# A hybrid RWKV-7 and attention step: norms, blocks, low-rank products and output products of the scan done in another way

## The chip, the cores and the metric

The program runs on one core of one Trainium2 chip. The metric is device time in microseconds (us) of one execution. The core has five engines, each with an instruction stream of its own that it works through in order: TensorE (PE in the profile; its weight loads are PEld) for matrix products into PSUM, VectorE (DVE), ScalarE (ACT), GpSimd (POOL, here called Pool) and SyncE (SP), which issues all the DMAs of this kernel.

## The reference, cut to what matters

Layer 0 is a bidirectional RWKV-7 scan beside a gated convolution, layer 1 is grouped-query attention. Of 1280 tokens 1024 are latent and 256 are context. What the change touches is the scan with its norms, and the mean squares of the other norms.

```python
def rwkv_scan(S0, r, w, k, v, kk, a, reverse):
    def step(S, inp):
        r_t, w_t, k_t, v_t, kk_t, a_t = inp
        sk = jnp.einsum('bhvk,bhk->bhv', S, kk_t)
        S = (S * w_t[:, :, None, :] - sk[..., None] * (kk_t * a_t)[:, :, None, :]
             + v_t[..., None] * k_t[:, :, None, :])
        return S, jnp.einsum('bhvk,bhk->bhv', S, r_t)
...
    w_log = -jax.nn.softplus(-(w0 + jnp.einsum('bldr,drc->bldc', jnp.tanh(lw), lw2))) - 0.5
    a = jax.nn.sigmoid(a0 + jnp.einsum('bldr,drc->bldc', la, la2))
    kk = kk / jnp.maximum(jnp.sqrt(jnp.sum(kk * kk, axis=-1, keepdims=True)), 1e-12)
    S_f, y_f = rwkv_scan(S0[:, 0], r_h, w_h[:, :, 0], k_h[:, :, 0], v_h, kk, a_h[:, :, 0], False)
    S_b, y_b = rwkv_scan(S0[:, 1], r_h, w_h[:, :, 1], k_h[:, :, 1], v_h, kk, a_h[:, :, 1], True)
    y = y_f + y_b
    mean = jnp.mean(y, axis=-1, keepdims=True)
    var = jnp.mean(jnp.square(y - mean), axis=-1, keepdims=True)
    y = ((y - mean) * lax.rsqrt(var + GN_EPS)).reshape(B, L, A_WIDTH) * lnx_g + lnx_b
```

## The kernel before, in words

**A planner orders the instructions.** Every part of the work is a Python generator. Before each piece it yields the engine that it needs and the tiles, rings of buffers (`Ring`) and conditions for which it waits. `Loom.run` (line 330) keeps a model of each engine's clock, with prices from `COST` (line 39), `TABLES` (line 46, the sets of ScalarE's functions; a change of set is priced at 1.28 us) and `Loom.issued` (line 246). It takes the first generator in the order of `PRECEDENCE` (line 48) whose turn has come by that model. The order of each engine's stream is thus fixed when the kernel is built. A price is used for that order alone; what an instruction waits for on the chip is set by semaphores. In the prices, two products whose 64 rows lie in different halves of the array run together when they are of type float32r.

**The stretch with the scan.** `fill` (line 1394) makes the first input projection: 34 column blocks, each as products of three kinds (high and low halves of activations and weights, `mm<-h_hi,whi` and the like in the profile) over three blocks of tokens. `evacuate` takes the results out of PSUM through ScalarE, VectorE and Pool; `norm_k` (line 715) normalises the keys in groups of 256 tokens, 20 times in all: square on ScalarE, a product with `ones2` on TensorE, Sqrt on ScalarE, a floor and a reciprocal on VectorE, a multiply, and a DMA to `rkv_d`.

The scan itself has 20 steps: four pairs of heads, and for each pair four groups of 256 latent tokens in both directions and one of the context. Each step passes through these generators:

- `prepare` (line 895): the low-rank products (`iv<-lor,lw`, for the two directions `d` one after the other, each in the single `iv` bank of PSUM, each with the parts `z` for decay and gate), tanh, cumulative decay, and the scaled operands on Pool.
- `interact` (line 981): products of the operands among themselves (`wk<-s,bk`, in both `wk` banks), masks, and the matrices to be inverted, which go through DRAM.
- `solve` (line 1041): the inverse of sixteen 32x32 triangles by 62 small VectorE operations on `acc` and `tmp`. Two solvers take the even and the odd steps; `all_solved` (line 1430) starts step n+2 only when the chain of step n is done.
- `merge` (line 1066): transposes the values, then joins the 32x32 inverses to 64x64 ones. The first blocks are transposed by 16 products of 32x32 with `ident` (`iv<-ident,w`), copied to `t11`, and followed by two more rounds of small products (`iv<-t,nn`, `iv<-w,zz`), each with a copy.
- `chain` (line 1121): four chunks of 64 tokens in sequence, both directions and both heads together. A chunk issues the product of state and keys (`ch<-hv,s`), copies it to `xs`, issues the first part of the outputs (`py<-s,hv`) and, on Pool, the decayed state `hg`; then the product with the inverse (`ch<-xs,w`), a copy to `hv`, the state product (`ch<-hv,tbk`), four VectorE operations that make the next state, the second part of the outputs (`py<-br,hv`), and the copy or addition of the outputs to `y`. Each direction has a `py` bank of its own; there are two.
- `finish` and `close_groups` (line 1241), 20 times: mean and variance of `y` by products with `ones2`, Sqrt on ScalarE, reciprocal on VectorE, and the gate.

**The other norms.** `norm_x` (line 1296) for the input rows, `rsqrt_mean` (line 1747) after each layer and `normed_heads` (line 1840) for queries and keys use a Sqrt on ScalarE and a reciprocal on VectorE, on 1 to 8 columns.

In the profile nearly every line is L145, that of the helper that records operations; tiles tell them apart. A float32 product stands as two records, so 160 records of `iv<-lor,lw` are 80 products.

Of the kernel before, what the change touches and what calls it, by code (L numbers as in the profile page):

```python
# [10 lines left out]
F32R = mybir.dt.float32r  # L11
AF = mybir.ActivationFunctionType
ALU = mybir.AluOpType
# [28 lines left out]

WINDOW = 3.413


TABLES = {AF.Tanh: 0, AF.Exp: 0, AF.Sqrt: 1, AF.Silu: 2}
# [70 lines left out]
class Loom:  # L117
# [128 lines left out]
    def issued(self, e, name, a, k, r):  # L246
# [9 lines left out]
        if e == "T":  # L256
# [3 lines left out]
            else:  # L260
                dur = max(0.054, n * (1 if ins[0].dtype == F32R else 4) / 2400.0)
                if ins[0].dtype == F32R and ins[0].partition_size() == 64:
# [20 lines left out]
        elif e == "G":  # L283
            dur = COST[e][0] + n * COST[e][1]
# [83 lines left out]
def hybrid_step(  # L368
# [34 lines left out]
    V.memset(eps_t[:, 0:1], EPS)  # L403
    V.memset(eps_t[:, 1:2], GN_EPS)

# [309 lines left out]
    def norm_k(p, b, f, done):  # L715

        t0, n, _ = BLK[b]
        for h in range(0, n, GRP):
# [176 lines left out]
    def prepare(x):  # L895
# [11 lines left out]
        for d in range(2):  # L907
            yield "T", x.lor, lw2, iv_ps
            pz = iv_ps.take()
            for z in range(2):  # L910
                T.matmul(pz[:, z * GRP:(z + 1) * GRP], lw2[HH[d], z, :], x.lor[HH[d], z, :], start=True, stop=True)
            for z in range(2):
# [3 lines left out]
            iv_ps.release(pz)  # L916
# [149 lines left out]
    def merge(x):  # L1066
# [54 lines left out]
    def chain(x):  # L1121
# [33 lines left out]
        yield "T", x.hv[:, :, :, 0], x.s[0], x.s[1], x.w, ch_ps  # L1155
        pc = ch_ps.take()
        for i in range(4):
# [46 lines left out]
            for d in range(2):  # L1204
# [4 lines left out]
                if d == 1:  # L1209
                    ysl = ysl[:, ::-1]  # L1210
# [1241 lines left out]
```

## Time and profile before

| | |
|---|---|
| median of 3 runs | 2253.53 us (2251.32 to 2257.36) |
| profiled execution | 2253.86 us |
| its span, first to last instruction | 2252.2 us |
| busy TensorE / VectorE / ScalarE / Pool | 2052.1 / 1471.9 / 1052.1 / 1012.0 us |
| mean granted TensorE clock | 0.951 |
| tables loaded by ScalarE | 56 in all, 71.8 us |

The table is for the whole execution; the stages have different limits, so the rows below are by stage and by tile. Busy times of an engine are the union of its instructions' times. The time of an instruction begins when its engine takes it up; where it then waits for a port, the wait is part of its time.

### The profile page before, as it was taken

How to read it: one execution, taken by the hardware profiler on the slowest of the kernel's cores; microseconds unless marked ns; L12 is line 12 of the kernel's file. 1: busy time of each engine (PE TensorE's matmuls, PEld its weight loads, DVE VectorE, ACT ScalarE, POOL GpSimd, SP SyncE). 2: the span in 40 equal slices, each digit the busy share in tenths (PEclk: the TensorE clock that was granted, in tenths of full speed). 3: DMA queues.
4: the chain of work that ended last, by engine and by line, in shares of the span. 5: the costliest groups of instructions: out<-in, count | busy, mean ns of one | idle time of the engine just before them, and what ended most of it. 6: DMA issues, size and time to landing. Idle time of an engine off the chain costs nothing.

```text
span 2252.2 us, 42921 instructions
## 1 busy us (share of the span) xinstructions
PE 2052.1 (91%) x15306; PEld 1411.7 (63%) x15306; DVE 1471.9 (65%) x3483; ACT 1052.1 (47%) x2476; POOL 1012.0 (45%) x1152
## 2 busy tenths in 40 slices
PE   4998889798988988998979999999999999999898
PEld 1486666576666666666657788888454545454487
DVE  2346878948888886868645733552877777775443
ACT  3446556645665556554435632221354444444422
POOL 2434344333344343333224321430487777888622
PEclk7999899999998999999889999999799999999899
DMA  7834344324433333342345633323321211102243
GB/s 271 305 98 131 98 105 131 85 68 114 102 97 103 99 96 101 85 111 54 86 153 185 206 111 88 99 87 107 82 53 48 60 42 38 43 28 71 58 131 108
DMA packets 337818, 232.86 MB, mean 103 GB/s; under 512 B 163890, under 2 KB 289860, under 8 KB 335556
## 3 DMA queue, kind: packets, MB, share of 16 engines
q1 hardware_dynamic: 337604, 230.12, 35.0%
q8 instruction: 120, 1.97, 0.4%
q14 instruction: 94, 0.77, 0.1%
HBM read 166.95 MB, written 57.75 MB: 100 GB/s over the span
## 4 chain that ended last, share of the span: by engine, by line
PE 39%; DVE 9%; DMA 5%; issue 3%; ACT 1%; POOL 1%; SPq 1%; DVEq 0%; POOLq 0%; ACTq 0%
PE mm L145 21%; PE pv L145 8%; PE wk L145 5%; PE py L145 4%; DVE mx L145 3%; DVE rz L145 1%; DVE zs L145 1%; DMA rz<-rz_d 1%; PE ch L145 1%; DVE tmp L145 1%; SPq L145 1%; DVE acc L145 1%; DMA rz_d<-rc 1%; DMA rc<-rz 0%; DVE hv L145 0%
## 5 line engine op out<-in xcount | busy, mean ns | idle before, releaser
L145 POOL TENSOR_TENSOR zs<-zs,pe 128x512 f32<-128x512 f32 x275 | 366.8, 1370 | 34.1 <-ACT pe L145 32.1
L145 PE MATMUL mm<-h_hi,whi 128*128 128x512 f32 (+1 forms) x816 | 336.5, 412 | 4.3 <-ACT whi L145 4.1
L145 PE MATMUL mm<-h_hi,wlo 128*128 128x512 f32 (+1 forms) x816 | 299.3, 367 | 8.1 <-DVE wlo L145 7.2
L145 PE MATMUL mm<-h_lo,whi 128*128 128x512 f32 (+1 forms) x816 | 298.7, 366 | 0.0
L145 POOL TENSOR_TENSOR wlo<-wraw,whi 128x128 fp32r<-128x128 f32 x228 | 111.4, 494 | 246.0 <-ACT whi L145 205.8
L145 PE MATMUL pv<-pe,v_sb 128*64 128x512 f32 (+1 forms) x832 | 200.4, 604 | 0.0
L145 PEld LDWEIGHTS mm<-h_hi,whi 128*128 128x128 f32 x816 | 159.9, 196 | 49.5 <-issue 12.2
L145 PEld LDWEIGHTS mm<-h_hi,wlo 128*128 128x128 f32 x816 | 160.1, 196 | 37.1 <-DVE wlo L145 10.0
L145 DVE TENSOR_TENSOR acc<-acc,tmp 128x60 f32<-128x60 f32 (+23 forms) x620 | 168.0, 273 | 20.8 <-issue 2.9
L145 PE MATMUL mm<-wts,omh 128*128 128x512 f32 x648 | 166.6, 410 | 7.6 <-ACT wts L145 4.0
L145 PEld LDWEIGHTS mm<-h_lo,whi 128*128 128x128 f32 x816 | 161.0, 197 | 14.4
L145 PE MATMUL mm<-wts,h_hi 128*128 128x512 f32 x480 | 151.1, 396 | 0.0
L145 POOL TENSOR_TENSOR hg<-hv,gc 64x128 f32<-64x128 f32 x152 | 65.1, 428 | 185.0 <-DVE hv L145 173.9
L145 PEld LDWEIGHTS mm<-wts,omh 128*128 128x128 f32 x648 | 122.9, 194 | 38.0 <-ACT wts L145 5.3
L145 ACT ACTIVATE whi<-wraw 128x128 fp32r<-128x128 f32 x272 | 80.2, 305 | 78.2 <-DMA wraw<-in_w_in_e_dram 40.3
L145 DVE TENSOR_REDUCE mx<-mm 128x1 f32<-128x512 f32 (+1 forms) x138 | 89.7, 660 | 36.7 <-PE py L145 12.6
L145 DVE SCALAR_TENSOR_TENSOR hv<-ch,gc,hg 64x64 f32<-64x64 f32 x288 | 81.3, 282 | 49.3 <-PE ch L145 42.2
L145 POOL TENSOR_TENSOR xr<-xr,og 128x512 f32<-128x512 f32 x40 | 54.6, 1364 | 128.4 <-DVE og L145 93.3
L145 PEld LDWEIGHTS pv<-pe,v_sb 128*64 128x64 f32 x832 | 51.6, 139 | 93.9 <-issue 82.3
L145 DVE TENSOR_REDUCE mx<-py 128x1 f32<-128x512 f32 (+1 forms) x138 | 89.6, 660 | 28.7 <-PE mm L145 13.0
L145 DVE TENSOR_TENSOR tmp<-acc,nra 128x31 f32<-128x31 f32 (+7 forms) x320 | 90.1, 282 | 27.4 <-DMA acc<-eye_d 17.7
L145 ACT ACTIVATE pe<-py 128x512 f32<-128x512 f32 (+1 forms) x139 | 79.1, 587 | 60.3 <-PE mm L145 20.3
(284 smaller groups left out, 5189.5 us busy)
## 6 DMA issues: line engine op xcount, KB each, us to landing
wraw<-in_w_in_e_dram SPq DMA_DIRECT2D x272, 64.0 KB
wada<-in_w_ada_dram SPq DMA_DIRECT2D x16, 1024.0 KB
inp<-rkv_d SPq DMA_DIRECT2D x40, 384.0 KB
om<-om_d SPq DMA_DIRECT2D x52, 256.0 KB
wraw<-in_w_in_o_dram SPq DMA_DIRECT2D x40, 256.0 KB
wada<-in_w_ada_dram SPq DMA_DIRECT2D x16, 512.0 KB
rkv_d<-nb SPq DMA_DIRECT2D x24, 256.0 KB
lor<-lora_d SPq DMA_DIRECT2D x40, 128.0 KB
```

What stands on the lines that cost most here:

```text
L145: r = f(*a, **k)
```

## The change

- **Norms.** Sqrt and reciprocal become a power of -0.5 on Pool (`ALU.pow`) with `minus_half` as exponent, in `norm_k`, `close_groups`, `norm_x`, `rsqrt_mean` and `normed_heads`. Scales go into the Square before; the epsilon is added by VectorE, or by an Identity on ScalarE in `close_groups`. The planner gets a price for it, `POW`, and no longer a set for Sqrt.
- **Low-rank products.** `prepare` issues the products of the two directions, which lie in the two row halves, alternately, into two banks (one `iv`, one `wk`); the planner prices two 64-row products of over 64 columns as running together, whatever their type.
- **Blocks.** `merge` transposes its first blocks with two VectorE transposes of 64x256.
- **Outputs.** In `chain`, the first part of a chunk's outputs follows the chunk's first product at once, both directions in one `py` bank. The second part (`by_u`) follows the next chunk's product with the inverse, and the copy or addition to `y` (`put`) the next chunk's new state; the last chunk's come at the end.

```diff
+POW = 8e-3
...
-TABLES = {AF.Tanh: 0, AF.Exp: 0, AF.Sqrt: 1, AF.Silu: 2}
+TABLES = {AF.Tanh: 0, AF.Exp: 0, AF.Silu: 1}
...
-                if ins[0].dtype == F32R and ins[0].partition_size() == 64:
+                if ins[0].partition_size() == 64 and ins[0].free_size() > 64:
...
-            dur = COST[e][0] + n * COST[e][1]
+            dur = COST[e][0] + n * (COST[e][1] + POW * (k.get("op") == ALU.pow))
...
-    V.memset(eps_t[:, 0:1], EPS)
     V.memset(eps_t[:, 1:2], GN_EPS)
+    minus_half = eps_t[:, 0:1]
+    V.memset(minus_half, -0.5)
...
-            yield "S", pt
-            S.activation(sq, pt[:, 0:GRP], AF.Sqrt)
+            yield "V", pt
+            V.tensor_scalar(out=sq, in0=pt[:, 0:GRP], scalar1=1e-24, scalar2=None, op0=ALU.max)
             wk_ps.release(pt)
-            yield "V", sq
-            V.tensor_scalar(out=sq, in0=sq, scalar1=1e-12, scalar2=None, op0=ALU.max)
-            yield "V", sq, 1.7
-            V.reciprocal(out=sq, in_=sq)
+            yield "G", sq
+            G.tensor_tensor(out=sq, in0=sq, in1=minus_half.broadcast_to([P, GRP]), op=ALU.pow)
...
-        for d in range(2):
-            yield "T", x.lor, lw2, iv_ps
-            pz = iv_ps.take()
-            for z in range(2):
+        yield "T", x.lor, lw2, iv_ps, wk_ps
+        pzs = [iv_ps.take(), wk_ps.take()]
+        for z in range(2):
+            for d, pz in enumerate(pzs):
                 T.matmul(pz[:, z * GRP:(z + 1) * GRP], lw2[HH[d], z, :], x.lor[HH[d], z, :], start=True, stop=True)
+        for d, pz in enumerate(pzs):
             for z in range(2):
...
-            iv_ps.release(pz)
+            (iv_ps, wk_ps)[d].release(pz)
...
-        yield "T", w8, iv_ps
-        pa = iv_ps.take()
-        for i in range(8):
-            for h in range(2):
-                r1 = 64 * h
-                T.matmul(pa[r1:r1 + 32, i * 32:i * 32 + 32], w8[r1:r1 + 32, i, 0:32], ident[r1:r1 + 32, r1:r1 + 32],
-                         start=True, stop=True)
+        yield "V", w8
         t11 = st1.tile([P, 256], F32, tag="t11", name="t11")
-        yield from copied(pa, *((t11[r:r + 32, :], pa[r:r + 32, 0:256]) for r in (0, 64)))
-        iv_ps.release(pa)
+        for rr in HH:
+            V.transpose(t11[rr].rearrange("p (i t) -> p i t", i=8), w8[rr, :, 0:32])
...
+        def by_u(i, py):
+
+            for d in range(2):
+                for h, rr in enumerate(HH):
+                    T.matmul(py[rr, d * C:d * C + C], x.hv[rr, h, d, i, :], x.br[rr, d, i, :], start=False,
+                             stop=(d == 1), skip_group_check=True)
+
+        def put(i, py):
+
+            for d in range(2):
...
+                yield "V" if add else "S", py, 0.3
...
+            py_ps.release(py)
+
-        yield "T", x.hv[:, :, :, 0], x.s[0], x.s[1], x.w, ch_ps
+        yield "T", x.hv[:, :, :, 0], x.s[0], x.s[1], x.w, ch_ps, py_ps
         pc = ch_ps.take()
+        before = None
...
                     T.matmul(pa[rr, d], x.s[h][:, d, i, 0, :], x.hv[:, h, d, i, :], start=True, stop=True)
+
+            py = py_ps.take()
+            for d in range(2):
+                for h, rr in enumerate(HH):
+                    T.matmul(py[rr, d * C:d * C + C], x.hv[:, h, d, i, :], x.s[h][:, d, i, 1, :], start=(d == 0),
+                             stop=False, skip_group_check=True)
             xs = chn.tile([P, 2, C], F32, tag="xs", name="xs", bufs=1)
             yield from copied(pa, (xs, pa))
-            yield "T", py_ps, py_ps
-            pys = [py_ps.take(), py_ps.take()]
-            for d in range(2):
-                for h, rr in enumerate(HH):
-                    T.matmul(pys[d][rr, 0:C], x.hv[:, h, d, i, :], x.s[h][:, d, i, 1, :], start=True, stop=False)
...
                     T.matmul(pu[rr, d], x.w[rr, d, i, :], xs[rr, d], start=True, stop=True)
+            if before:
+                by_u(i - 1, before)
             yield from copied(pu, *((x.hv[rr, h, :, i, :], pu[rr]) for h, rr in enumerate(HH)))
...
-            yield ("T",)
-            for d in range(2):
-                for h, rr in enumerate(HH):
-                    T.matmul(pys[d][rr, 0:C], x.hv[rr, h, d, i, :], x.br[rr, d, i, :], start=False, stop=True)
...
+            if before:
+                yield from put(i - 1, before)
+            before = py
             if i < 3:
-                yield "T", x.hv[:, :, :, i + 1]
+                yield "T", x.hv[:, :, :, i + 1], py_ps
+        yield ("T",)
+        by_u(3, before)
+        yield from put(3, before)
...
-            S.activation(sq, y, AF.Square)
+            S.activation(sq, y, AF.Square, scale=C ** -0.5)
...
-            S.activation(sq, pm[:, 0:GRP], AF.Sqrt, scale=1.0 / C, bias=eps_t[:, 1:2])
+            S.activation(sq, pm[:, 0:GRP], AF.Identity, bias=eps_t[:, 1:2])
             iv_ps.release(pm)
-            yield "V", sq
-            V.reciprocal(out=sq, in_=sq)
+            yield "G", sq
+            G.tensor_tensor(out=sq, in0=sq, in1=minus_half.broadcast_to([P, GRP]), op=ALU.pow)
...
-        V.tensor_tensor(out=ss[:, 2:3], in0=ss[:, 0:1], in1=ss[:, 1:2], op=ALU.add)
-        yield "S", ss
-        S.activation(ss[:, 2:3], ss[:, 2:3], AF.Sqrt, scale=1.0 / D, bias=eps_t[:, 0:1])
-        yield "V", ss
-        V.reciprocal(out=ss[:, 2:3], in_=ss[:, 2:3])
+        V.tensor_scalar(out=ss[:, 2:3], in0=ss[:, 0:1], scalar1=ss[:, 1:2], scalar2=EPS, op0=ALU.add, op1=ALU.add)
+        yield "G", ss
+        G.tensor_tensor(out=ss[:, 2:3], in0=ss[:, 2:3], in1=minus_half, op=ALU.pow)
```

## Rows read from the trace of the kernel before

**Rows 1.** Stages: length, busy us of PE, PEld, DVE, ACT, POOL, granted clock
```profile
270.00:1110.00 840.00, 753.27 (x8273) 555.13 (x8272) 664.24 (x1977) 464.31 (x1245) 326.80 (x551) 0.96 0.36 94
...
1171.00:1310.00 139.00, 133.19 (x602) 105.77 (x602) 83.11 (x170) 82.74 (x183) 53.96 (x39) 0.98 0.57 181
1310.00:1575.00 265.00, 263.38 (x1236) 215.79 (x1234) 109.95 (x195) 65.08 (x138) 60.81 (x52) 1.00 0.31 97
```

**Rows 2.** Tiles hv, whi: count, ns min/median/max, first and last start
```profile
L145 PE MATMUL ch<-hv,s x640: 222/222/370, 272.9 to 1157.1; 128*64 128x64 f32 x160
...
L145 PE MATMUL mm<-h_hi,whi x816: 274/393/988, 64.4 to 1110.1; 128*128 128x512 f32 x110, 128*128 128x256 f32 x54
```

**Rows 3.** Timeline of TensorE, chains 17 to 19: start, us, instructions
```profile
1055.25 0.45 PE L145 MATMUL ch<-hv,s 128*64 128x64 f32 x8
...
1076.81 0.45 PE L145 MATMUL py<-br,hv 64*64 64x64 f32 x8
...
1128.20 0.69 PE L145 MATMUL iv<-ident,w 32*32 32x32 f32 x32 [0.56 <-ACT sqy L145]
...
1140.09 0.70 PE L145 MATMUL ch<-hv,s 128*64 128x64 f32 x8
```

**Rows 4.** Chain of waits that ended last: start, us, what
```profile
1082.95 2.32 DMA acc<-eye_d
...
1119.51 4.77 DMA w_d<-acc
```

**Rows 5.** Tiles sqy and sq: count, ns min/median/max, first and last start
```profile
L145 DVE RECIPROCAL sqy<-sqy x20: 1739/1745/1754, 388.0 to 1165.4; 128x256 f32<-128x256 f32 x20
L145 POOL TENSOR_TENSOR y<-y,sqy x20: 723/736/1087, 389.8 to 1167.7; 128x256 f32<-128x256 f32 x20
...
L145 DVE RECIPROCAL sq<-sq x20: 1727/1752/1755, 138.1 to 670.8; 128x256 f32<-128x256 f32 x20
```

**Rows 6.** ScalarE's groups, 91 to 1116 us: count, busy us, mean ns, idle before
```profile
L145 ACT ACT_TABLE_LOAD x46 | 59.0, 1283 | 0.8
```

**Rows 7.** Timeline at 1198 us; then tiles sums and acc
```profile
1198.24 1.60 POOL L145 TENSOR_TENSOR h_lo<-tl,h_hi 128x512 fp32r<-128x512 f32 x1 [0.30 <-DVE tl L145]
...
1198.73 1.13 DVE L145 TENSOR_TENSOR sums<-sums 128x1 f32<-128x1 f32 x1
...
L145 DVE TENSOR_TENSOR sums<-sums x20: 147/159/1256, 1172.8 to 2246.9; 128x1 f32<-128x1 f32 x20
...
L145 DVE TENSOR_TENSOR acc<-acc,tmp x620: 121/221/1048, 203.0 to 1119.3; 128x60 f32<-128x60 f32 x15, 128x54 f32<-128x54 f32 x10, 128x28 f32<-128x28 f32 x10, 128x48 f32<-128x48 f32 x9
```

**Rows 8.** Timeline of TensorE: low-rank products in the scan; scores in attention
```profile
657.87 1.13 PE L145 MATMUL iv<-lor,lw 64*128 64x256 f32 x4
...
1640.47 0.39 PE L145 MATMUL wk<-ql,kh 64*128 64x512 f32 x1
1640.47 0.39 PE L145 MATMUL mm<-ql,kh 64*128 64x512 f32 x1
```

**Rows 9.** Timeline of TensorE in merge 18; then tiles t and mt
```profile
1083.33 0.69 PE L145 MATMUL iv<-ident,w 32*32 32x32 f32 x32
...
1085.53 0.69 PE L145 MATMUL iv<-t,nn 32*32 32x32 f32 x32
...
L145 ACT ACTIVATE t<-iv x36: 357/374/377, 252.1 to 1129.3; 32x256 f32<-32x256 f32 x36
L145 DVE COPY t<-iv x4: 412/418/422, 574.7 to 768.3; 32x256 f32<-32x256 f32 x4
...
L145 DVE STREAM_TRANSPOSE mt<-mx x24: 193/211/213, 1590.5 to 2066.8; 128x32 f32<-128x32 f32 x24
```

**Rows 10.** Timeline of TensorE, first chunk of chain 18
```profile
1091.79 0.45 PE L145 MATMUL ch<-hv,s 128*64 128x64 f32 x8
...
1093.06 0.45 PE L145 MATMUL py<-s,hv 128*64 128x64 f32 x8
1093.44 0.45 PE L145 MATMUL ch<-xs,w 64*64 64x64 f32 x8
```

More of the change, by code (lines that the diff above doesn't have):

```diff
@@ L1153, in chain @@
                 ch_ps.release(pt)
-        yield "T", x.hv[:, :, :, 0], x.s[0], x.s[1], x.w, ch_ps
+        def by_u(i, py):
[5 more added lines that the diff above has]
+            for d in range(2):
+                c0 = i * C if d == 0 else GRP - (i + 1) * C
+                ysl = y[d][:, c0:c0 + C]
+                if d == 1:
+                    ysl = ysl[:, ::-1]
+                add = (j is not None and j >= 2) or c0 in seen
+                yield "V" if add else "S", py, 0.3
+                if add:
+                    V.tensor_tensor(out=ysl, in0=py[:, d * C:d * C + C], in1=ysl, op=ALU.add)
+                else:
+                    S.activation(ysl, py[:, d * C:d * C + C], AF.Copy)
+                if j is None:
+                    seen.add(c0)
+            py_ps.release(py)
+        yield "T", x.hv[:, :, :, 0], x.s[0], x.s[1], x.w, ch_ps, py_ps
         pc = ch_ps.take()
+        before = None
         for i in range(4):
@@ L1199, in chain @@
                                                in1=hg[rr, d], op0=ALU.mult, op1=ALU.add)
-            yield ("T",)
-            for d in range(2):
-                for h, rr in enumerate(HH):
-                    T.matmul(pys[d][rr, 0:C], x.hv[rr, h, d, i, :], x.br[rr, d, i, :], start=False, stop=True)
-            for d in range(2):
-                py = pys[d]
-                yield "V" if j is not None and j >= 2 else "S", py, 0.15
-                c0 = i * C if d == 0 else GRP - (i + 1) * C
-                ysl = y[d][:, c0:c0 + C]
-                if d == 1:
-                    ysl = ysl[:, ::-1]
-                if (j is not None and j >= 2) or c0 in seen:
-                    V.tensor_tensor(out=ysl, in0=py[:, 0:C], in1=ysl, op=ALU.add)
-                else:
-                    S.activation(ysl, py[:, 0:C], AF.Copy)
-                if j is None:
-                    seen.add(c0)
-                py_ps.release(py)
+            if before:
+                yield from put(i - 1, before)
+            before = py
             if i < 3:
-                yield "T", x.hv[:, :, :, i + 1]
+                yield "T", x.hv[:, :, :, i + 1], py_ps
+        yield ("T",)
+        by_u(3, before)
+        yield from put(3, before)
         ch_ps.release(pc)
@@ L1299, in norm_x @@
             t = ldp.tile([P, D], F32, tag="xq", name="xq")
-            S.activation(t, xts[i], AF.Square, accum_out=ss[:, i:i + 1])
-        yield "S", ss
-        S.activation(ss[:, i0:i0 + n], ss[:, i0:i0 + n], AF.Sqrt, scale=1.0 / D, bias=eps_t[:, 0:1])
+            S.activation(t, xts[i], AF.Square, scale=D ** -0.5, accum_out=ss[:, i:i + 1])
         yield "V", ss
-        V.reciprocal(out=ss[:, i0:i0 + n], in_=ss[:, i0:i0 + n])
+        V.tensor_scalar(out=ss[:, i0:i0 + n], in0=ss[:, i0:i0 + n], scalar1=EPS, scalar2=None, op0=ALU.add)
+        yield "G", ss
+        G.tensor_tensor(out=ss[:, i0:i0 + n], in0=ss[:, i0:i0 + n], in1=minus_half.broadcast_to([P, n]), op=ALU.pow)
         for i in range(i0, i0 + n):
@@ L1742, in evac @@
             yield "S", x
-            S.activation(og, x, AF.Square, accum_out=sums[self.l][:, i, h:h + 1])
+            S.activation(og, x, AF.Square, scale=D ** -0.5, accum_out=sums[self.l][:, i, h:h + 1])
             R["og"].release(og)
@@ L1846, in normed_heads @@
         t3 = t.rearrange("p (h d) -> p h d", d=C)
-        S.activation(t, pt, AF.Square)
+        S.activation(t, pt, AF.Square, scale=C ** -0.5)
         yield "V", t
         V.tensor_reduce(out=ss, in_=t3, axis=AX.X, op=ALU.add)
-        yield "S", ss
-        S.activation(ss, ss, AF.Sqrt, scale=1.0 / C, bias=eps_t[:, 0:1])
         yield "V", ss
-        V.reciprocal(out=ss, in_=ss)
+        V.tensor_scalar(out=ss, in0=ss, scalar1=EPS, scalar2=None, op0=ALU.add)
+        yield "G", ss
+        G.tensor_tensor(out=ss, in0=ss, in1=minus_half.broadcast_to([P, nh]), op=ALU.pow)
         yield "V", ss
```

2 lines of the change are left out of this document (1 added, 1 removed).

## The prediction

> **What bounds the kernel now.** The windows by stage come first [rows 1]. Almost all that the diff touches lies in the stretch from 270 to 1110 us, where the scan over 20 steps runs and the products of the first input projection fill the rest of TensorE. The reader is to see that nothing is full there: of 840.00 us TensorE is busy 753.27 (90%), VectorE 664.24 (79%), ScalarE 464.31 (55%), Pool 326.80 (39%), at a granted clock of 0.96, nearly always the upper level of 2.4 GHz. From 1310 to 1575 us TensorE is busy 263.38 of 265.00 us, so what the diff does to other engines there costs nothing.
>
> With no engine full, a loop of dependences sets the pace. The tile views give its period [rows 2, 3]: the first chain starts at 272.9, the last at 1140.09, so 19 steps take 867.2 us, 45.6 each. Two solvers work in turn, and step n+2 may be solved only when chain n is through (`all_solved`), so one trip round is two steps, 91.3 us, and the scan holds 9.5 trips. One trip can be read off [rows 3, 4]: chain 17 starts at 1055.25 and issues its last output product at 1076.81; the next solver's start matrix is fetched at 1082.95; its solution is stored at 1119.51; the 32-column inverse begins at 1128.20; chain 19 starts at 1140.09. That is 22 us of chain, 6 until the fetch, 37 of solve, 9 of DMA, 12 of merge. The filling products start last at 1110.1 [rows 2], before chain 19 starts: the scan ends last, so work taken off TensorE shortens the stage only where it shortens a trip.
>
> **The norms (power on Pool).** `norm_k` and `close_groups` run 20 times each on 128x256, 40 norms or 4 a trip. Each loses a VectorE reciprocal of 1.75 us [rows 5], 70 us in all, and the change of ScalarE's table: 46 loads between 91 and 1116 us take 59.0 us [rows 6]. `norm_k` also loses its Sqrt; in `close_groups` an Identity takes the Sqrt's place, and the floor in `norm_k` stays one VectorE pass, now out of PSUM. Added is a Pool power on 128x256. No row shows one. The nearest below is Pool's multiply of the same tile, 0.74 us. From above: the VectorE reciprocal is 4.2 times a plain pass over 256 columns (1745 against 418 ns, [rows 5, 9]), and 4.2 times 0.74 is 3.07 us. The planner's own price in the diff is 0.15 + 256 x 0.0101 = 2.74 us; its formula without the power gives 0.69 where the row has 0.736, so I take 2.74.
>
> What the planner doesn't price is the port. At 1198.24 Pool runs a tensor operation of 1.60 us; a VectorE add of one column starts at 1198.73 and takes 1.13 us, ending as Pool does, though the median of its kind is 159 ns [rows 7]. The solver's adds, with both inputs in SBUF, go from 221 ns in the median to 1048 [rows 7]. So Pool holds VectorE up for whole instructions. The reciprocals, 1727 to 1755 ns, never waited for anybody [rows 5]. A power thus gives back 1.75 us of VectorE and blocks it for b. If it holds the port throughout, b is 2.74 us times the chance that VectorE has work that needs the port; it is busy 79% of the time, mostly in the 62 small solver operations of each step, so I take b = 2.2; bounds 0 (the power leaves the port free) and 3.07.
>
> The Trainium skill, page "GPSIMD Engine Reference", section 3.1, says that data-dependent branching on Pool costs about 12 cycles an element. At that page's 1.2 GHz this would be 2.6 us for 256 elements, an estimate of 3.3 us for the power with the multiply of the row added; b would be 2.6 and the result about 2245 us. No run here shows such a branch.
>
> In Pool's queue a power delays what stands behind it, `hg` of the chain and the halves of the weights among them; `hg` is needed only after two products and two copies, and the weights have nine buffers, so I cost this at nothing; without that cover it is up to 2.74 us whenever a chunk meets a power. The write of `norm_k` stays behind its norm on SP's queue, where a late norm would hold up the loads behind it; with a power as long as Sqrt, table load and reciprocal together I cost this at nothing too.
>
> **Blocks turned by VectorE.** Each merge loses 16 products of 32x32 (32 records) and a copy: from 1083.33 to the next product at 1085.53, 2.20 us, of which 0.69 are the products, 0.37 the copy and 1.14 hand-overs [rows 9]. Added are two VectorE transposes of 64x256. Bounds: 0.21 us, a transpose of 32 columns, and eight times that, 1.7 us; I take 0.42, a VectorE pass over 256 columns [rows 9]. The path is then 0.84 and half the hand-overs, 1.4 us: 0.8 us gained a trip (by the bounds, 1.2 gained to 1.8 lost). VectorE gets 1.7 us more a trip, since the copies were nearly all on ScalarE.
>
> **Low-rank products in row halves.** Two products with 64 rows take 1.13 us [rows 8], twice a step. In attention, products on the two row halves start at the same time, at 1640.47 [rows 8]. If that holds here, a step saves up to 1.0 us of TensorE, 20 us in all; if not, nothing. They belong to a later step and only stand in the chain's way: I take 0.3 us a trip. The second half now asks for one of two `wk` banks, which `interact` needs in pairs; the single `iv` bank is taken once instead of twice. I cost the exchange at nothing.
>
> **Outputs with the next chunk's inverse.** No product is removed. In a chunk, the first output products at 1093.06 stand between the chain's product at 1091.79 and the inverse at 1093.44 [rows 10]. Now they follow the chain's product at once, and the second output products go where TensorE waits for a copy. So fewer places are left where filler slips in. The most that can be gained is both groups' 0.38 us, 0.76 a chunk; the least is nothing; I take 0.4, 1.6 us a trip of four chunks. A new wait: the bank of chunk i-1 is freed only after VectorE's (or ScalarE's) add late in chunk i, and the first output products of chunk i+1 wait for it, with the inverse queued behind on TensorE; but that waits for its own copy anyway, so nothing, or 0.35 us a chunk if the add is late.
>
> **ScalarE.** Without 59 us of table loads, a copy of the loop finds a load before it less often: 59.0 of 1025 us is 5.8%, half a load (0.64 us) each time, over some 22 ScalarE steps a trip: 0.8 us. The mean squares in the later stages (`rsqrt_mean`, `normed_heads`) swap a short Sqrt and reciprocal for a Pool power of 1 to 8 columns; they lie beside a TensorE that is 96% busy or more [rows 1], so nothing, or about 1 us for each of ten tiles in the stretch from 1171 if it waits behind a Pool operation.
>
> **The sum.** Gains a trip: 0.8 + 0.8 + 0.3 + 1.6 = 3.5 us; 9.5 trips make 33 us. VectorE a trip: 4 x (2.2 - 1.75) + 1.7 = 3.5 us more; half of it, an estimate, falls on work the trip waits for, since the other solver and the filling also use VectorE: 1.75 us, times 9.5 is 17 us. Net: 16.6 us less. The profiled execution took 2253.86 us (2252.2 of span and 1.7 around it), 0.3 above the median of the runs. I predict 2237 us.
>
> **The rivals.** First, the power doesn't hold the port, b = 0. VectorE then gains 5.3 us a trip, half of it 25 us in all, and the time is 2253.9 - 33 - 25 = 2195. For it: the power computes more than it reads. Against: every Pool tensor operation in the trace blocks whole. Second, the hold eats the gain: with b = 3.07, what the reciprocal's ratio gives with VectorE blocked every time, the loss is (4 x 1.32 + 1.7) / 2 x 9.5 = 33 us, and the time stays at 2254. Third, slower: the same mechanism, decided at b = 3.08, where the loss a trip equals the gain of 3.5. At a power of 4.0 us, blocked throughout, the loss is 51 us and the time 2271. For it: the row of 1048 ns and that the plan, which knows no port, will queue solver work right behind powers. Against: the planner's price of 2.74. Last, the row halves don't run together: 3 us are lost, 2240, inside the forecast.
>
> **How the numbers follow.** About 0.3%, 7 us, is what a measurement of this kernel can tell from no change. Forecast (2222 to 2247, the failed halves included) 0.40; free port (below 2222) 0.20; gain eaten (2247 to 2260) 0.18; slower 0.22. So faster 0.60, same 0.18, slower 0.22. The range goes from 2195 to 2268, which leaves out the tails of the free port and of the slow case, about 0.09 each.
>
> **What would show it.** In the profile of the changed kernel: a row of Pool powers on 128x256, with its mean; solver operations of up to that length beside it, and their median; the table loads down to a few; the low-rank products in pairs with one start; transposes of about 0.4 us; the scan's period from the starts of the chain's first product, 45.6 us now and about 44.7 if I am right. A period of 43 or less with solver operations that don't lengthen means the free port; a power above 3 us with a period over 45.6 the slow rival. The prediction is also wrong if the loop isn't what sets the scan's end, which an earlier end of the filling with an unchanged last chain would show.

## The result and the profile after

| | before | after |
|---|---|---|
| median | 2252.43 us (2248.52 to 2257.36) | 3746.55 us (3743.61 to 3750.1) |
| span of the profiled execution | 2252.2 us | 3743.8 us |
| mean granted TensorE clock | 0.951 | 0.764 |
| busy TensorE / VectorE / ScalarE / Pool | 2052.1 / 1471.9 / 1052.1 / 1012.0 us | 2077.2 / 1453.8 / 945.8 / 2687.1 us |

The ratio is 1.6632, with a 95% interval from 1.6595 to 1.6669. I had forecast 2237 us, in a range up to 2268, and faster with a chance of 0.60. The change cost 1494 us.

TensorE and VectorE have about as much work as before, ScalarE 106 us less, and Pool has 1675 us more. The tile views (as [rows 5]: count, ns min/median/max, first and last start) name it:

```profile
L148 POOL TENSOR_TENSOR sqy<-sqy,eps_t x20: 41115/41117/41577, 959.8 to 2609.6; 128x256 f32<-128x256 f32 x20
...
L148 POOL TENSOR_TENSOR sq<-sq,eps_t x20: 41115/41127/41498, 138.3 to 1569.0; 128x256 f32<-128x256 f32 x20
```

A power on 128x256 takes 41.1 us, where my sum had 2.74. The 40 of them are 823.5 + 822.9 = 1646.4 us of Pool, and they are spread from 138 to 2650 us. The scan is stretched over the same time (as [rows 1, 2]):

```profile
658.00:2660.00 2002.00, 800.55 (x7997) 600.38 (x7996) 680.16 (x2075) 418.99 (x1214) 1555.44 (x557) 0.68 0.17 44
```
```profile
L148 PE MATMUL ch<-hv,s x640: 221/222/370, 657.8 to 2600.0; 128*64 128x64 f32 x160
...
L148 PE MATMUL mm<-h_hi,whi x816: 277/395/988, 65.6 to 2360.5; 128*128 128x512 f32 x110, 128*128 128x256 f32 x54
```

The first chain starts at 657.8 instead of 272.9, and the last product of state and keys at 2600.0 instead of 1157.1. Pool is busy for 78% of this stage, TensorE for 40%, at a granted clock of 0.68 instead of 0.96: much of it at the lower level, 1.2 GHz. From that last product to the end it is 1144 us, against 1095 before: nearly all of the loss lies ahead of it, in the stretch with the scan.

How a power on Pool stops TensorE is seen in the timeline of the chain (start, us, instructions, idle time before and what ended it):

```profile
1748.81 41.12 POOL L148 TENSOR_TENSOR sqy<-sqy,eps_t 128x256 f32<-128x256 f32 x1
1790.01 0.72 POOL L148 TENSOR_TENSOR y<-y,sqy 128x256 f32<-128x256 f32 x1
1790.69 0.94 POOL L148 TENSOR_TENSOR hg<-hv,gc 64x128 f32<-64x128 f32 x2
...
1757.04 0.60 PE L148 MATMUL wk<-s,bk 64*64 64x128 f32 x14
1791.99 0.69 PE L148 MATMUL ch<-hv,tbk 128*64 128x64 f32 x8 [34.35 <-ACT hv L148]
...
1791.12 0.27 ACT L148 ACTIVATE hv<-ch 64x128 f32<-64x128 f32 x1 [35.28 <-POOL hg L148]
...
1790.77 0.60 DVE L148 SCALAR_TENSOR_TENSOR y<-y,lnx,bon 128x256 f32<-128x256 f32 x1 [34.90 <-POOL y L148]
1791.29 0.42 DVE L148 TENSOR_TENSOR tmp<-acc,nrb 128x60 f32<-128x60 f32 x1
```

Three engines stand still for 34 us behind one power. Pool works through its queue in order, so the chain's `hg`, 0.94 us of work, starts when the power and the multiply of `y` behind it are through. ScalarE's copy to `hv` waits for `hg`: in the kernel it writes over the same part of `hv`, `x.hv[rr, h, :, i, :]`, from which `hg` reads the state. TensorE's state product waits for that copy. VectorE has an instruction at the head of its own queue that needs the `y` which the power scales, and the solver's next operation, `tmp<-acc,nrb`, stands behind it. The view of waits begins with these; a wait of the filling products for halves of the weights (`wlo`), which Pool makes too, stands further down (us in total, times, longest):

```profile
DVE y L148 <- POOL y L148: 676.3, 18, 43.0
DVE nb L148 <- POOL sq L148: 645.7, 17, 41.3
PEld ch L148 <- ACT hv L148: 410.3, 35, 38.7
ACT hv L148 <- POOL hg L148: 406.0, 24, 38.1
...
PEld mm L148 <- POOL wlo L148: 110.6, 6, 38.1
```

The other parts do what the diff says. ScalarE loads 3 tables instead of 56; the blocks are turned in 0.44 us, where I took 0.42; the low-rank products of the two halves run in pairs with one start (as [rows 6, 8, 9]):

```profile
L148 ACT ACT_TABLE_LOAD x3 | 3.8, 1283 | 3.8 <-DMA eye_d<-eye 3.0 <-PEq L2450 0.8
```
```profile
L148 DVE STREAM_TRANSPOSE t<-w x40: 412/436/445, 634.4 to 2492.2; 64x256 f32<-64x256 f32 x40
```
```profile
2275.58 0.48 PE L148 MATMUL iv<-lor,lw 64*128 64x256 f32 x1
2275.58 0.48 PE L148 MATMUL wk<-lor,lw 64*128 64x256 f32 x1
...
2276.33 0.38 PE L148 MATMUL iv<-lor,lw 64*128 64x256 f32 x1
2276.34 0.38 PE L148 MATMUL wk<-lor,lw 64*128 64x256 f32 x1
```

A step's eight records end at 2276.72, 1.14 us after the first start, against 2 x 1.13 us in [rows 8].

### The profile page after: what moved, and what is told of

Same layout as the page of the kernel before. It is cut to its first block, busy times and chain, and to the rows that moved or that the text cites. A ratio compares the mean times of both kernels' runs of the same rounds, so it can differ in the third digit from the quotient of the medians.

```text
span 3743.8 us, 41657 instructions
## 1 busy us (share of the span) xinstructions
PE 2077.2 (55%) x14666; PEld 1443.2 (39%) x14666; DVE 1453.8 (39%) x3514; ACT 945.8 (25%) x2317; POOL 2687.1 (72%) x1187
## 4 chain that ended last, share of the span: by engine, by line
POOL 29%; PE 26%; DVE 10%; issue 6%; DMA 2%; ACT 2%; SPq 0%; POOLq 0%; DVEq 0%; ACTq 0%
POOL sqy L148 21%; PE mm L148 12%; PE pv L148 5%; POOL sq L148 5%; PE wk L148 4%; PE py L148 3%; DVE mx L148 2%; PE ch L148 1%; DVE acc L148 1%; DVE tmp L148 1%; PE iv L148 1%; DVE hv L148 1%; DVE ta L148 1%; DVE rz L148 1%; POOL ssh L148 1%
## 5 line engine op out<-in xcount | busy, mean ns | idle before, releaser
L148 POOL TENSOR_TENSOR sqy<-sqy,eps_t 128x256 f32<-128x256 f32 x20 | 823.5, 41174 | 38.9 <-ACT sqy L148 36.0
L148 POOL TENSOR_TENSOR sq<-sq,eps_t 128x256 f32<-128x256 f32 x20 | 822.9, 41145 | 29.1 <-DVE sq L148 27.6
L148 PE MATMUL mm<-h_hi,wlo 128*128 128x512 f32 (+1 forms) x816 | 316.8, 388 | 263.6 <-DVE wlo L148 155.0
L148 DVE SCALAR_TENSOR_TENSOR y<-y,lnx,bon 128x256 f32<-128x256 f32 x20 | 16.9, 846 | 676.3 <-POOL y L148 676.3
L148 DVE SCALAR_TENSOR_TENSOR nb<-nb,par,sq 128x256 f32<-128x256 f32 x20 | 16.6, 832 | 645.7 <-POOL sq L148 645.7
L148 PE MATMUL ch<-hv,tbk 128*64 128x64 f32 x608 | 38.9, 257 | 400.9 <-ACT hv L148 400.4
L148 POOL TENSOR_TENSOR wlo<-wraw,whi 128x128 fp32r<-128x128 f32 x166 | 80.9, 494 | 165.9 <-ACT whi L148 138.9
L148 PEld LDWEIGHTS ch<-hv,tbk 128*64 128x64 f32 x608 | 27.5, 156 | 424.4 <-ACT hv L148 410.3
L148 DVE TENSOR_TENSOR acc<-acc,tmp 128x60 f32<-128x60 f32 (+24 forms) x620 | 173.3, 280 | 20.9 <-issue 2.5
L148 ACT ACTIVATE hv<-ch 64x128 f32<-64x128 f32 x160 | 43.4, 271 | 464.4 <-POOL hg L148 406.0
L148 PE MATMUL wk<-sq,ones 128*128 128x256 f32 x40 | 19.8, 590 | 224.4 <-ACT sq L148 188.2
L148 PE MATMUL wk<-ident,bk 128*128 128x128 f32 x160 | 29.7, 317 | 191.4 <-DVE br L148 153.9
```

Source lines behind the costliest of these rows:

```text
L148: r = f(*a, **k)
```

## The experiments

In the tables below, "planner" is the latest of the planner's own engine clocks when it has placed its last piece, in us. It isn't a time on the chip and leaves out what precedes the planner, so only its differences are compared. "omh" is the first start of the output projection's products (`mm<-wts,omh`), which begin when scan and filling are nearly through.

**What a power costs.** Unused powers were put ahead of the kernel before:

```diff
+    for n in (8, 32, 64, 128, 256):
+        power(f"cols{n}", n)
+    power("parts64", p=64)
+    power("parts32", p=32)
+    power("half_e", e=0.5)
+    power("two_e", e=2.0)
...
+    nc.gpsimd.tensor_tensor(out=gate2, in0=fa, in1=fa, op=ALU.mult)
+    nc.vector.tensor_tensor(out=beside, in0=gate2, in1=fa, op=ALU.add)
...
+        nc.vector.tensor_tensor(out=beside, in0=beside, in1=fa, op=ALU.add)
```

> The kernel before with a row of unused Pool powers put ahead of all its work, to price the operation by itself: 8, 32, 64, 128 and 256 columns on 128 partitions, 256 columns on 64 and 32 partitions, exponents 0.5, 2 and 1, bases 1 and 1e-6, an exponent from a full tile; then additions of 128x256 on VectorE beside a power, and beside 16 multiplications of 128x512. Theory (a fixed price a column, whatever the values, since the 40 powers of the changed kernel lie within 41115 to 41577 ns, and 8 columns took 1744 ns): 5.4, 10.5, 20.8 and 41.1 us for 32, 64, 128 and 256 columns, the same for all exponents and bases and for fewer partitions. Rival 1 (price goes with elements): 20.6 us with 64 partitions, 10.3 with 32. Rival 2 (price goes with the values): exponents 1 and 2 or base 1 much below 41.1. VectorE's additions: theory (a power leaves the port free) as long beside the power as alone, about 0.33 to 0.42 us; rival (it holds the port) one addition as long as the power. Beside the multiplications an addition takes up to a whole multiplication, 1.3 us or more. Total time 300 to 700 us above the kernel before.

It took 3169.49 us, 911 more than before and outside the 300 to 700 expected, since the row holds more powers than I had added up. Pool's groups (count, busy us, mean ns, idle before; `of_small` has a base of 1e-6 where the others have 3):

```profile
L423 POOL TENSOR_TENSOR cols<-base,e 128x256 f32<-128x256 f32 x2 | 82.2, 41120 | 0.0
L423 POOL TENSOR_TENSOR parts<-base,e 32x256 f32<-32x256 f32 x2 | 82.2, 41107 | 0.0
L423 POOL TENSOR_TENSOR one_e<-base,e 128x256 f32<-128x256 f32 x2 | 82.2, 41107 | 0.0
L423 POOL TENSOR_TENSOR of_small<-basesmall,e 128x256 f32<-128x256 f32 x2 | 82.2, 41107 | 0.0
...
L423 POOL TENSOR_TENSOR cols<-base,e 128x128 f32<-128x128 f32 x2 | 41.4, 20719 | 0.0
...
L423 POOL TENSOR_TENSOR cols<-base,e 128x32 f32<-128x32 f32 x2 | 10.8, 5417 | 0.0
L423 POOL TENSOR_TENSOR cols<-base,e 128x8 f32<-128x8 f32 x2 | 3.3, 1644 | 1.0 <-DVE e L412 1.0
```

The price goes with the columns alone: (41.107 - 1.644) / 248 = 0.159 us a column and 0.37 beside. A quarter of the partitions, an exponent of 1, a small base: the same 41.1 us (and 41.2 with the exponent from a full tile). Both rivals fall. For the port, VectorE's additions with both inputs in SBUF beside the power that ran from 860.74 to 901.85:

```profile
860.81 0.82 DVE L452 TENSOR_TENSOR beside<-gate,fa 128x256 f32<-128x256 f32 x1 [40.72 <-POOL gate L451]
861.55 0.41 DVE L447 TENSOR_TENSOR side<-side,fa 128x256 f32<-128x256 f32 x1
861.89 0.41 DVE L456 TENSOR_TENSOR beside<-beside,fa 128x256 f32<-128x256 f32 x1
```

The first, which starts with the power, takes 0.4 us longer; from there they follow at 0.34 us each. Beyond its start the power doesn't hold the port. (They were through before the multiplications began, so nothing is learnt of those here.)

**The powers alone.** The kernel before with the norms' part of the diff and nothing else:

> The kernel before with the norms alone changed to powers on Pool, nothing else. Theory (the power accounts for all of the loss): 3720 to 3800 us, with the 40 wide powers at 41.1 us each, 1646 us on Pool. Rival (part of the loss comes from the power together with the regrouped outputs, whose banks come free later): at least 100 us below the changed kernel's 3746, so under 3650.

3808.80 us, 9 above the theory's range: the norms alone account for the whole loss, and 62 us more than that. What the other parts are worth beside 1646 us of powers isn't read from one run each.

**The width of the power**, with the order of all instructions as in the changed kernel. Only the first columns get norms of their own, which then stand for the others too:

```diff
-            G.tensor_tensor(out=sq, in0=sq, in1=minus_half.broadcast_to([P, GRP]), op=ALU.pow)
+            G.tensor_tensor(out=sq[:, 0:WIDE], in0=sq[:, 0:WIDE], in1=minus_half.broadcast_to([P, WIDE]), op=ALU.pow)
```

> The changed kernel with each of the 40 powers over 128 of the 256 columns, the norms of the first 128 tokens used for all (so the norms of the other half aren't computed); planner's order unchanged. A power then takes 20.7 us, the 40 of them 829 instead of 1646. Theory A (each power stands in the way of the scan for its whole length, as the loss of 1494 us over 40 powers, 37 us each, has it): 40 x 20.4 us less, about 2930 us. Theory B (Pool's busy time alone is the bound: 327 + 829 us of Pool work fit into about 1160 us): 2253 + 290 to 350, about 2570.

> The changed kernel with each of the 40 wide powers over 32 of the 256 columns, the norms of the first 32 tokens used for all (so the other norms aren't computed); planner's order unchanged. A power then takes 5.4 us, twice the 2.74 that I took. Theory A (a power costs its whole length whatever the length, 40 x 15.3 us less than with 128 columns): about 2317 us. Theory B (a power of a few us hides in the chain's other waits): 2296 us, the time without powers, or less.

> The changed kernel, its order unchanged, with each of the 40 wide powers over 16 of the 256 columns, the norms of the first 16 tokens used for all (so the other norms aren't computed). By the rows a power then takes 2.92 us, nearly the 2.74 that my forecast of 2237 us took. Theory A (linear to the end, 40 x 2.5 us below the 2312 us of the run at 5.4 us): 2212. Theory B (at this length the other parts of my sum decide): 2237 if the sum is right, 2280 or more if the shifted order costs here what it cost in the runs without powers.

| columns | a power, us | time, us | less than the row above / 40 times the power's shortening, us |
|---|---|---|---|
| 256 | 41.1 | 3746.55 | |
| 128 | 20.7 | 2929.32 | 817 / 816 |
| 32 | 5.4 | 2311.89 | 617 / 612 |
| 16 | 2.9 | 2246.98 | 65 / 101 |

Down to 5.4 us a power costs its whole length, 40 times; Pool's sum of work (1160 us with 128 columns) isn't the bound, since that theory had 2570. (256 and 16 columns have several runs, 128 columns one, and 32 columns two that lie 15 us apart.) At the last step some 0.6 of the length is left, and the time lies 35 us above theory A's 2212. The last row also comes near to what my forecast of 2237 us was about, a power of 2.74 us: with powers of 2.9 us it takes 2246.98 us, a ratio of 0.998 (0.996 to 1.000).

**The price told to the planner:**

```diff
-POW = 8e-3
+POW = 0.158
```

> The changed kernel with the planner's price of a power set to what it takes, 0.158 us a column more instead of 0.008 (POW); the operations are the same, only their order and the choice between engines change. Theory A (Pool's busy time sets the stage: 1635 of 2100 us between 300 and 2400, and its idle 465 us there come from the wrong order): up to 465 us less, 3280 to 3550. Theory B (each power blocks the scan's chain whatever the order, since the norms and the chain's decayed state share Pool's queue): within 100 us of 3746.

3579.18 us, between the two theories: the order dealt with the true price gives back 167 of the 1494 us.

**The three other parts.** First all of them, without powers; then one at a time, each the kernel before with its hunks of the diff:

> The changed kernel with all its norms put back to Sqrt and reciprocal; row halves, turned blocks and regrouped outputs stay. Theory (the power alone, at 41.1 us instead of the 2.74 I took, made the kernel slow; the other terms of my sum hold): gains of 1.6 + 0.8 + 0.3 us a trip, 26 us over 9.5 trips, less half of 1.7 us of VectorE a trip, 8 us: about 2235 us, between 2220 and 2250. Rival 1 (one of the other parts adds a wait of its own, the bank of chunk i-1 above all): 2260 or more. Rival 2 (the three parts lie beside the path): 2246 to 2260, as before.

> The kernel before with the regrouped outputs alone. The three parts beside the powers together cost 37 us, where my sum had them gain 18. Theory A (the regrouping is what costs: the chains take as long as before, 20.5 us each, the filling products end 90 us earlier, and TensorE then runs at half clock): 2285 to 2310 us, filling products ended by 1050. Theory B (it gains what my sum said, 1.6 us a trip, 15 us, and another part costs): about 2243. Theory C (the plan around it is shuffled without direction): within 15 us of 2258.

> The kernel before with the low-rank products alone changed: alternately from the two row halves into an iv and a wk bank, and the planner's price for it. My sum: 0.3 us a trip, 3 us less, so 2250 to 2262. Rival (the wk bank that it takes is missing to the products of the operands, and the planner's new price moves the filling): 2270 or more. In the trace: products of the two halves with one start, if they run together.

> The kernel before with the blocks alone turned by VectorE. My sum: 0.8 us a trip gained, half of 1.7 us of VectorE a trip lost, so nothing, 2250 to 2262. Rival (two transposes of 0.44 us wait in VectorE's queue behind the solvers' operations, which the TensorE products never did): some 3 us a merge that the trip waits for, 6 a trip, 55 us: 2300 or more.

The run of all three misses my theory (2235) and the rival by which they lie beside the path (2246 to 2260). In the order that the planner then deals, each costs by itself, and together they cost no more than one of them:

| | time, us | ratio (95% interval) | planner | omh |
|---|---|---|---|---|
| before (its runs beside these) | 2258 to 2259 | | 1889 | 1123.6 |
| all three | 2295.68 | 1.0155 (1.0116 to 1.0193) | 1940 | 1181.1 |
| outputs | 2293.56 | 1.0144 (1.0115 to 1.0172) | 1934 | 1167.8 |
| row halves | 2277.70 | 1.0089 (1.0058 to 1.0121) | 1898 | 1145.8 |
| blocks | 2301.00 | 1.0168 (1.0133 to 1.0202) | 1909 | 1171.5 |

The places differ. With the outputs alone the chains run as before, from 266.0 to 1149.7, 883.7 us against 884.2 in [rows 2], but the filling ends at 1152.4 instead of 1110.1, at a granted clock of 0.90 instead of 0.96 (kernel with the outputs, the views of [rows 1, 2]):

```profile
270.00:1110.00 840.00, 728.88 (x8003) 547.76 (x8004) 663.39 (x1956) 450.85 (x1213) 314.31 (x530) 0.90 0.36 93
```
```profile
L145 PE MATMUL mm<-h_hi,whi x816: 274/394/988, 63.5 to 1152.4; 128*128 128x512 f32 x110, 128*128 128x256 f32 x54
```

With all three or the blocks alone it is the other way round: the filling is used up by 1020.1 or 1061.5, and the chains go on alone to 1219.1 or 1222.8. So it isn't one wait that all of them bring; theory A of the outputs had the filling end early, and it ended late. That pointed at the order.

**The order alone.** Two shifts of the planner's numbers in the kernel before leave all the work as it is. What changes is the order and what the planner chooses with it: the engine of some copies (with the first shift 10 of the 80 copies to `xs` are VectorE's, 4 before) and ScalarE's table loads (54 and 64, against 56):

```diff
-COST = {"V": (0.065, 1.04e-3), "S": (0.06, 0.833e-3), "G": (0.15, 2.1e-3)}
+COST = {"V": (0.065, 1.02e-3), "S": (0.06, 0.833e-3), "G": (0.15, 2.1e-3)}
```
```diff
-        return 0.2 if a == "T" else 0.14
+        return 0.2 if a == "T" else 0.15
```

> The kernel before with one number of the planner changed, VectorE's price a column from 1.04 to 1.02 ns: the operations stay, their order shifts. Theory A (the order of before is a lucky or a tuned one, and any shift of it costs about what the three parts did, 18 to 41 us, by a filling that leaves TensorE idle and its clock low for longer): 2270 to 2300 us, granted clock below 0.945. Theory B (the operations of the three parts themselves cost): within 10 us of the kernel before.

> The kernel before with another number of the planner changed, the delay it counts between two engines other than TensorE, from 0.14 to 0.15 us: the operations stay, their order shifts. Theories as for the shift of VectorE's price: A 2270 to 2300 us, B within 10 us of the kernel before. One of the two near before and one above it would mean that a plan's luck is about as large as the three parts' effects.

2298.22 us, ratio 1.0170 (1.0137 to 1.0203), and 2296.80 us, 1.0179 (1.0152 to 1.0205). A 2% change of one planning price costs as much as the three parts. By the planner's clock these two orders end at 1909 and 1930 us, and before at 1889, earlier than any of the other small shifts that were planned for it (1890 to 1994). For the three parts without powers the earliest of 30 shifts ends at 1888. Two more were run, the order of the three parts with the earliest end and the earliest of the shifts of before:

> The three other parts without powers, as in the first of these runs (2296 us), with the planner's lead for VectorE's pieces at 0.05 instead of 0.10 us: of 30 small shifts the order with the earliest end by the planner's own clock, 1888 us against 1940 for the first run's order and 1889 for the kernel before. Theory A (the three parts are worth about nothing by themselves, and the 37 us were the order): 2240 to 2270 us. Theory B (the parts cost): 2285 or more. Theory C (they gain what my sum said, and the order hid it): 2235 or less.

> The kernel before with the planner's delay between two engines other than TensorE at 0.13 instead of 0.14 us: the second earliest of 30 orders of the unchanged operations, 1890 us by the planner's own clock against 1889 for the order of before itself, which is the earliest of them; the rest lies between 1902 and 1994. Theory A (that clock tells a good part of what the order does): 2245 to 2270 us. Theory B (the order of before is lucky in a way that the clock doesn't tell): 2280 to 2300, as the two other shifts.

2263.64 us, ratio 1.0029 (1.0011 to 1.0048), and 2256.17 us, 0.9988 (0.9969 to 1.0007). So in the order that the planner's clock has as the best, the three parts cost 0.3%, and the 1.55% of the first run was mostly its order. A gain as large as my sum gave them doesn't show in either order; what they are worth apart from the order is smaller than what the order does, and isn't measured more closely than that. The rival for the blocks, 3 us a merge in VectorE's queue, had 2300 us and met it (2301.00), but falls as the cause: the run of 2264 us turns its blocks in the same way, and no run shows that the two other parts give 40 us back.

**A power on four columns.** Since the price goes with columns, the sums can be laid out with tokens on the partitions. The same edit sets the planner's price to 0.158 and moves the multiply of `y` by its norm from Pool to VectorE:

```diff
-            T.matmul(pt[:, 0:GRP], ones2, sq, start=True, stop=True)
+            for u in range(2):
+                T.matmul(pt[:, 2 * u:2 * u + 2], sq[:, u * P:(u + 1) * P], ones2[:, 0:P:64], start=True, stop=True)
...
-            G.tensor_tensor(out=sq, in0=sq, in1=minus_half.broadcast_to([P, GRP]), op=ALU.pow)
+            G.tensor_tensor(out=nr, in0=nr, in1=minus_half.broadcast_to([P, 4]), op=ALU.pow)
+            yield "V", nr
+            V.tensor_copy(sq.rearrange("p (q c) -> p q c", q=4), nr.unsqueeze(2).broadcast_to([P, 4, C]))
...
+                T.matmul(pt[:, u * P:(u + 1) * P], sq[:, u * P:(u + 1) * P], ident, start=True, stop=True)
```

> The kernel before with all norms by powers, but none on more than 8 columns: the sums of squares of 256 tokens and two heads are made by two products with the squares as weights, so that they lie as 128x4; floor or epsilon, power (about 1.0 us by the row of 128x4 in the changed kernel), a VectorE copy that spreads them to 128x256, and two products with the identity that turn them back. The planner gets the measured price, 0.158 us a column more. Theory (the price goes with columns only, and the blocking with the price): 40 powers at 1.0 us, nothing of the 1494 us left; VectorE loses 40 reciprocals of 1.75 us and gains 40 copies of about 0.4; ScalarE loses 59 us of table loads; TensorE gains some 40 x 0.5 us: 2230 to 2290, the plan's luck included. Rival (even a short power stands in the way): above 2300.

> The changed kernel with its norms by powers on at most 8 columns, as in the run of the four columns, and the measured price in the planner; row halves, turned blocks and regrouped outputs are kept. Theory A (orders of the planner scatter by 1 to 2% on the chip, and the planner's own clock tells part of it: 1889 us for before, 1898 to 1940 for the shifted ones, which took 18 to 41 us longer; here it says 1872): 2235 to 2260 us. Theory B (the three parts cost by themselves, about 37 us together): 2290 or more.

> The same with VectorE's price a column at 1.03 instead of 1.04 ns, of 30 such small shifts of the planner's numbers the one with the earliest end by the planner's own clock, 1851 us. Theory A: 38 us below before by that clock, so 2210 to 2240 us on the chip. Theory B (that clock tells nothing of the chip): 2250 to 2300.

> The same with the planner's delay from TensorE to another engine at 0.19 instead of 0.20 us, third earliest of the 30, 1868 us by the planner's own clock. Theory A: 2225 to 2255 us; theory B: 2250 to 2300.

| | time, us | ratio (95% interval) | planner | omh |
|---|---|---|---|---|
| before + these norms | 2271.64 | 1.0071 (1.0047 to 1.0096) | 1913 | 1147.6 |
| the whole change with them | 2235.34 | 0.9913 (0.9879 to 0.9947) | 1872 | 1094.6 |
| the same, VectorE's price 1.03 | 2216.57 | 0.9841 (0.9814 to 0.9868) | 1851 | 1083.4 |
| the same, TensorE's delay 0.19 | 2240.53 | 0.9943 (0.9922 to 0.9964) | 1868 | 1117.9 |

All three orders of the whole change are faster than before, by 12 to 36 us; the third row beats both kernels, by 36 and by 1530 us. Its norms (first with their powers) and its scan:

```profile
L148 POOL TENSOR_TENSOR nry<-nry,eps_t x20: 1007/1014/1470, 372.3 to 1130.3; 128x4 f32<-128x4 f32 x20
L148 DVE COPY sqy<-nry x20: 278/391/1369, 373.4 to 1131.3; 128x256 f32<-128x256 f32 x20
```
```profile
L148 PE MATMUL ch<-hv,s x640: 222/222/369, 277.2 to 1121.1; 128*64 128x64 f32 x160
```

The state products go from 277.2 to 1121.1, 844 us against 884 in [rows 2]. That the planner's clock doesn't tell everything is seen in the first row: 1913 us, hardly other than the 1909 of a shifted before, but 27 us less on the chip.

## Why the prediction was wrong

**The step that failed is the price of the power.** I had bounds from 0.74 to 3.07 us and took 2.74; it is 41.1, 13 times the upper bound. The lower end came from a multiply on the same engine, the upper from VectorE's ratio of reciprocal to plain pass: neither row is of a power, and I had no reason why the ratio on one engine should hold on another. The value between was the planner's price, which the diff itself brought. As the planner's formula agreed with a row for the multiply, I trusted its other term, for which no row stood. 40 x (41.1 - 2.74) = 1534 us is the error; the width runs show that this is what was lost, at one us for each us of power.

The estimate beside it, from the Trainium skill ("GPSIMD Engine Reference", section 3.1, some 12 cycles an element for data-dependent branching), gave 3.3 us. The measurement differs by a factor of 12, and the exponent of 1 or a base of 1 took as long as any other.

**Pool's queue, costed at nothing, is where it went.** I named the place rightly: `hg` behind a power, up to a power's length whenever a chunk meets one. But I thought `hg` was needed only after two products and two copies; the row of ScalarE's copy, which waits for `hg` for 406.0 us in 24 cases, shows that it is needed a copy earlier, before the copy overwrites what it reads. I didn't name the other half: the multiply that waits for the power stands in VectorE's queue ahead of the solvers (676.3 and 645.7 us). The weights' halves, which I also put at nothing, kept the filling waiting (110.6 us). Between 2.9 and 5.4 us of power the time still grew by some 0.6 us for each, so "nothing" is doubtful at my own price too; no run has a shorter power in this layout.

**The port.** b = 2.2 was wrong: the row of additions beside a power shows 0.4 us at its start and nothing after. The first rival's free port was right in its mechanism, and worth nothing at this price. The third rival had the sign, with a power above 3.08 us, but by the port, so it gave 2271. In the changed kernel the solver's operations confirm that the power leaves the port free. The first two lines lie beside the power that started at 1748.81, the last two beside a plain multiply on Pool (start, us):

```profile
1748.86 0.65 DVE L148 TENSOR_TENSOR tmp<-acc,nra 128x72 f32<-128x72 f32 x1
...
1749.64 0.22 DVE L148 TENSOR_TENSOR acc<-acc,tmp 128x72 f32<-128x72 f32 x1
...
1791.71 0.73 POOL L148 TENSOR_TENSOR bk<-kds,cum 128x256 f32<-128x256 f32 x1
1791.74 0.77 DVE L148 TENSOR_TENSOR acc<-acc,tmp 128x60 f32<-128x60 f32 x1
```

Of the solver's operations on `acc` and `tmp`, 274 ran wholly inside a power, later than 1 us after its start: 215 ns in the median and 239 at most, the same as those that ran away from Pool's operations. Of those that started inside a plain Pool operation of over 0.5 us, with more than 0.3 us of it left, all end 0.02 to 0.10 us after it, 127 in this kernel and 127 in the one before. So "blocks whole" was right for the operations that the trace then had, and wrong for the power.

The Trainium skill ("SBUF — State Buffer", section "SBUF: two separate sides") says that whichever of a Pool operation that reads SBUF and a VectorE operation with two SBUF inputs starts first gets the shared ports for the whole instruction. [rows 7] and the 127 agree for plain Pool operations; for the power the additions at 0.34 us beside 41.1 differ, and the measurement decides.

**The three other parts.** Their sizes were right: transposes 0.436 us (0.42 taken), row halves in pairs, 1.1 us less a step (up to 1.0), table loads from 71.8 to 3.8 us. What failed is the way from them to the time. I gave the regrouped outputs 1.6 us a trip, and the state products took 883.7 us instead of 884.2; I took the order as given, so that a saving on the path arrives. In none of the runs of these parts alone or together, without powers, did it: the planner deals the whole stage anew after each edit, and in the two shifts that alone moves the time by 38 and 40 us, five times the 7 us that I called measurable and more than my whole sum of 16.6. Nor is the loop always what ends the scan: with the outputs alone the filling ended after the chains. In their best order by the planner's clock the three parts cost 6 us where I had a gain of 26 less 8. (The trip that I read off runs from 1055.25 to 1140.09, 84.8 us, the last one; the mean is 91.3. The sum uses only the number of trips, so nothing hangs on it.)

**The sum at my own price.** The changed kernel with powers of 2.9 us took 2247, 10 us above my forecast. That isn't a confirmation but luck as far as is known. The order of the changed kernel ends early by the planner's clock (1852), and b, the cover of `hg` and the way from the parts to the time were wrong in the sum; which of them make up for each other wasn't measured.

**What stays open.** How much of the gain of the four columns is due to the removed reciprocals, how much to the 68 us of table loads and how much to the order wasn't taken apart. Nor was it found what in an order lets the clock fall; in the slower orders it is 0.89 to 0.94 from 270 to 1110 us, in before 0.96, but the kernel of 2216 us has 0.94 there as well.

## What to carry to other kernels

A price for which no row stands has no bounds from other operations, least of all from the diff's own planning table: a run of the operation alone would have settled this case. An operation in an in-order queue that also feeds the critical chain can cost its whole length, as here from 5.4 us up, however idle that engine is on average. Where a planner deals the instructions, an edit of 1% has to be compared over several orders, before and after, or the order's luck is taken for the edit's effect.

## What the runs showed of the hardware

- A Pool power in float32 takes 0.159 us a column plus 0.37, the same for 128, 64 and 32 partitions, for exponents -0.5, 0.5, 1 and 2 and for three bases (1e-6, 1, 3); Pool's multiply of `y` on 128x256 takes 0.72 us.
- VectorE's additions with two SBUF inputs run at full pace beside a power (0.34 us each), but for 0.4 us at its start, although plain Pool operations hold them until their end (all 127 of the solver's in either kernel that start inside one with over 0.3 us of it left).
- The same work in the order that a 2% change of one planning price makes takes 1.7% longer here.
